# Hybrid decoder block in fp32 pieces: another issue order in the passage from the output projection to the up projection

## The chip, the core and the metric

The kernel runs on one core of one Trainium2 chip. The metric is the device time in microseconds. Five engines work side by side, each through its own list of instructions in a fixed order: TensorE (PE in the profile, with its weight loads as PEld), VectorE (DVE), ScalarE (ACT), GpSimd (POOL) and SyncE (SP, which here only issues transfers).

## What is computed

The reference is one transformer block on 512 tokens of width 1024, all in float32:

```python
h = rmsnorm(x, norm_attn_g)
u = h @ w_in                                    # q, k, v, pool input, gates
a = diff_attention(q, k, v, positions, lam, subln_g, lam_init)
p = multiscale_pool(u_pool, w_pool, pool_scale)
x = x + (sigmoid(g_A) * a + sigmoid(g_P) * p) @ w_out
h2 = rmsnorm(x, norm_mlp_g)
z = square(relu(h2 @ w_up))                     # 1024 -> 4096
x = x + z @ w_down                              # 4096 -> 1024
return rmsnorm(x, final_norm_g)
```

The change concerns the lines from `x + ... @ w_out` to the first part of `h2 @ w_up`.

## The kernel before, in words

**Products in three terms.** Every float32 operand is split into a high part (a cast to the multiplier's format, on ScalarE) and a low part (operand minus high part, on VectorE). A product is then three matmuls: high by high, high by low, low by high. For a weight tile of 128 by 1024 this split is `split_w`: the cast at L112, the subtraction at L113.

**Output projection.** `po` accumulates the left 512 output columns for four row tiles of 128 tokens (t = 0 to 3) in four PSUM banks at once (L605 to L610). The right 512 columns follow row tile by row tile in the loop from L625: 8 slices k of the inner dimension, three matmuls each (`mm_rows`, L581 to L583), into bank 4 + t. The four weight tiles `ws` of the right half are split just ahead of that loop (L619 to L622).

**What follows each row tile.** As soon as row tile t is finished, `x1_add` adds the residual (L587, VectorE) and squares with a row sum (L561, ScalarE). `row_scale` makes the inverse root of the mean square with one step of refinement (L571 to L573 on ScalarE, L574 and L575 on VectorE). L636 multiplies the row tile by its scale and by the gain: this is `h2`, in two buffers used in turn. Eight transposes on TensorE (L644, tile `h2T`) turn it into two PSUM banks with the features on the partitions.

**The up projection's forms.** The MLP's products use Strassen's scheme (Winograd's form): the inputs are split in two by features and in two by tokens, and seven products, called A11, A12, S1, S2, S3, A22 and S4, take the place of eight. A11 and A12 need the first two row tiles alone: their operands are the cast and the subtraction at L656 and L657. The other forms need row tiles 2 and 3 as well. For t = 2 and 3 the loop copies a transposed bank (L649), adds and subtracts (L650), and makes the operands of S1 and S2 (`forms_h2`, L596 for the difference, L602 for the cast, L603 for the low part).

**The products of `up(0)`.** `product` runs one form: for i in 0, 1 (two weight tiles, two output banks) and p in 0, 1 (halves of a bank) four high-by-high and high-by-low pairs (L775, L778) and then four low-by-high matmuls (L781), each with 256 columns. One form is 48 matmuls. In `up(0)` the order of the forms is A11, A12, S1, S2, S3, A22, S4. The weights come from the generator `weights`: A11's are block 0 (`b11`), A12's block 2 (`b21`), and S1's a sum in the buffer pair `ga`. `parts` does the splitting. For S1 its casts are ordered behind the last `row_scale` (L729). After S1's split the next block is added onto `ga` by an accumulating transfer that GpSimd issues (`plus`, L685): the sum is the weight of S2. Outputs of A11 are kept at L803, and A12's are added to them at L807 (`join`).

**What sets the order of the work.** The scheduler takes, for each engine, the ready instruction that stands earliest in the program, by a simulated clock of its own, and so writes down one fixed order per engine. `after(later, earlier)` adds a constraint for two instructions of one engine: in that engine's list the first comes behind the second. It adds no wait between engines. The constraints around the change are these, before:

- the first matmul of row tile t of the right half comes behind the last of row tile t - 1, for t = 1, 2, 3 (L629);
- the transposes of row tile 0 come behind the end of row tile 1's matmuls, those of row tile 1 behind the end of row tile 2's (L631 to L633);
- the transposes of row tile 2 come behind the second quarter of A11 (L785), those of row tile 3 behind the second quarter of A12 (L788);
- the casts of A11's and A12's weights (`b11`, `b21`, two tiles each) have no constraint.

Of the kernel before, what the change touches and what calls it, by code (L numbers as in the profile page):

```python
# [51 lines left out]
def block_kernel(ctx, tc, xT, x_tok, gains, pos, consts, w_in, w_v, w_pool, w_out, w_up, w_dn, out):  # L52
# [10 lines left out]
    state = {}  # L63
# [153 lines left out]
    for n in range(2):  # L217
        accs = [bank((0, 1, 2, 3, 4, 5, 6, 0)[4 * n + t], f"v{n}_{t}") for t in range(NT)]
        for kk in range(4):
# [7 lines left out]
            for k2 in range(2):  # L227
# [4 lines left out]
                k = 2 * kk + k2  # L232
# [11 lines left out]
            if n == 0 and 0 < kk < 3:  # L244
                i = kk - 1
# [287 lines left out]
    A11, A12, A22, A21, S1, S2, S3, S4 = range(8)  # L533
# [34 lines left out]
    def row_scale(t, n):  # L568

        src, r, u = (st[:, t, i : i + 1] for i in (n, 4, 5))  # L570
        A.activation(out=r, in_=src, func=AF.Ln, scale=1.0 / D, bias=st[:, t, 2:3])  # L571
        A.activation(out=r, in_=r, func=AF.Exp, scale=-0.5)
        state["rows"] = A.activation(out=u, in_=r, func=AF.Square, scale=1.0 / math.sqrt(D))  # L573
        V.scalar_tensor_tensor(out=u, in0=src, scalar=st[:, t, 3:4], in1=u, op0=ALU.add, op1=ALU.mult)  # L574
        V.scalar_tensor_tensor(out=r, in0=u, scalar=-3.0, in1=r, op0=ALU.add, op1=ALU.mult)  # L575
        return r
# [48 lines left out]
    for t in range(NT):  # L625
        a_ = bank(4 + t, f"po1_{t}")
        for k in range(NK):
            m, end = mm_rows(a_, t, k, ws[k // 2], k == 0, k == NK - 1)
            if t and k == 0:  # L629
                after(m, state["po"])  # L630
        if 0 < t < 3:  # L631
            for b in range(2):
                after(state["h2T", t - 1, b], end)  # L633
        state["po"] = end
        x1_add(t, 1, a_)
        V.scalar_tensor_tensor(out=h2[:, t % 2], in0=x1[:, t, :], scalar=row_scale(t, 1), in1=g2b, op0=ALU.mult, op1=ALU.mult)  # L636
        pv = []
        for b in range(2):
            pt = bank((t % 2) * 2 + b, f"h2T{t}_{b}")
            for j in range(4):  # L640
                k = 4 * b + j
                if j == 1:
                    state["h2T", t, b] = state["h2T"]
                state["h2T"] = T.transpose(out=pt[:, j * P : j * P + P], in_=h2[:, t % 2, k * P : k * P + P], identity=ident)  # L644
            pv.append(pt.rearrange("p (j q) -> p j q", q=P))
        sl = slice((t % 2) * P, (t % 2) * P + P)
        if t > 1:

            A.copy(out=hw[:, 1, :, sl], in_=pv[0])  # L649
            V.tensor_tensor(out=hw[:, 0, :, sl], in0=pv[1], in1=hw[:, 1, :, sl], op=ALU.subtract)  # L650
            forms_h2((S1, S2), sl)
        if t == 3:
            forms_h2((S3,), slice(0, HS))
        for b in range(t // 2, 2):
            hi, lo = (gab[b][:, t // 2, i, :, sl] for i in range(2))
            A.copy(out=hi, in_=pv[b])  # L656
            part = V.tensor_tensor(out=lo, in0=pv[b], in1=f(hi), op=ALU.subtract)  # L657
            if t == 3:
                after(part, state[S3])
            if t < 2:  # L660
                A.copy(out=h2f[:, b, :, sl], in_=pv[b])
# [8 lines left out]
    def weights(src, q, nm, order):  # L670

        def raw(b, tag="wr", pool=wp):
            if b == 2:
                both = big.tile([P, 2, 1024], F32, tag="s1b", name=f"wr21_{nm}{q}")
                tiles = [both[:, c] for c in range(2)]
            else:
                tiles = [pool.tile([P, 1024], F32, tag=tag, name=f"{tag}_{nm}{b}_{q}_{c}", bufs=2) for c in range(2)]
            if b is not None:
                for c in range(2):
                    nc.sync.dma_start(out=tiles[c], in_=src[q, b, c])  # L680
            return tiles

        def plus(tiles, b):

            return [G.dma_start(out=tiles[c], in_=src[q, b, c], accum_op=ALU.add) for c in range(2)]  # L685

        def parts(rs, b, hold=None, add=None):

            third = nparts[0] % 3 == 2
            nparts[0] += 1  # L690
            out_ = []
            for c in range(2):
                hi, lo = (
                    (bk if third else wp).tile([P, 1024], F32R, tag=t_ + "b" * third, name=f"{t_}_{nm}{b}_{q}_{c}", bufs=2 if third else 4)
                    for t_ in ("wh", "wl")
                )
                if add is None:
                    cast = split_w(rs[c], hi, lo, eng=V)
                else:

                    cast = A.copy(out=hi, in_=rs[c])
                    A.mul(out=lo, in_=f(hi), mul=-1.0)
                    G.dma_start(out=lo, in_=src[q, add, c], accum_op=ALU.add)
                if hold:
                    after(cast, hold)
                out_.append((hi, lo))
            return out_

        early = nm == "u" and q == 0
        r11, al, ga = raw(0), raw(1, "wal", bk), raw(None, "wga", bk)  # L710
        for c in range(2):
            if early:
                nc.sync.dma_start(out=ga[c], in_=src[q, 0, c])
            else:
                V.tensor_tensor(out=ga[c], in0=r11[c], in1=al[c], op=ALU.add)
        if early:
            plus(ga, 1)
            plus(al, 3)
        for n, form in enumerate(order):
            if form == A11:  # L720
                yield parts(r11, "b11", zhi[q, S1] if nm == "d" and q else None)
            elif form == A12:
                yield parts(raw(2), "b21", zhi[q, A11] if nm == "d" and q else None)
            elif form == S4:
                yield parts(raw(3), "b22", None, 3 if nm == "d" and q == 3 else None)
            elif form == S3:
                yield parts(al, "t3", first[-1])
            else:
                w = parts(ga, f"t{form}", state["rows"] if form == S1 and early else None if form == S1 else first[-1])  # L729
                if form != A22:  # L730
                    adds = plus(ga, {S1: 3, S2: 2}[form])
                if form == S1 and not early:

                    for i in plus(al, 3):
                        after(i, adds[1])
                yield w
# [23 lines left out]
    def up(q):  # L760
# [3 lines left out]
        def product(form, name, onto=None):  # L764
# [3 lines left out]
            for i in range(2):  # L768
                hi, lo = w[i]
                for p in range(2):  # L770
# [11 lines left out]
                        if q == 0 and form == A12 and (i, p, k) == (1, 0, 0):  # L782
                            after(m, state["h2T"])
                    if q == 0:
                        if (form, i, p) == (A11, 0, 1):  # L785
                            for b in range(2):
                                after(state["h2T", 2, b], m)
                        elif (form, i, p) == (A12, 0, 1):  # L788
                            for b in range(2):
                                after(state["h2T", 3, b], m)  # L790
                        if form != A11 or i + p:
                            after(begin, state["um"])
                        state["um"] = m
# [226 lines left out]
```

## Time and profile before

| what | before |
|---|---|
| median of three runs | 676.74 us (676.6 to 678.25) |
| the profiled execution's own time | 677.01 us |
| its span, first to last instruction | 675.1 us |
| PE busy | 664.3 us (98%) |
| DVE busy | 529.7 us (78%) |
| ACT busy | 461.6 us (68%) |
| POOL busy | 122.3 us (18%) |
| granted TensorE clock, mean | 0.997 |

All times in the views are microseconds from the start of the span. The stretch that the change touches runs from about 326 us (left half of the output projection ends) to about 371 us (third product of the up projection ends). Buffer numbers are left out of tile names: `po` is any of the output projection's banks, `um` any bank of an up product, `wh_ub` and `wl_ub` the high and low parts of a block's weights (`b11`, `b21`, `b22`), `wh_ut` and `wl_ut` those of a sum's weights (S1, S2 and so on), `gss` an operand of S1 to S4, `rawz` the buffer of kept products. In a row of the timeline the columns are start, duration, engine, line, operation, output and inputs, count, and in brackets the idle time of the engine ahead of it with what ended it. Matmuls follow one another every 0.12 us in `um` (256 columns) and every 0.23 us in `po` (512 columns).

### The profile page before, as it was taken

The page shows a single profiled execution, that of the slowest core. Times are in us where ns is not written, and L with a number is a line of the kernel's source. Part 1 is how long each engine was busy: PE and PEld are TensorE (multiplying, and loading weights), DVE is VectorE, ACT ScalarE, POOL GpSimd, SP SyncE. Part 2 cuts the span into 40 slices and gives each one's busy share as a digit, 9 for nine tenths or more (in the row PEclk, how much of TensorE's full clock was granted, in tenths as well). Part 3 has the DMA queues.
Part 4 walks back from the last instruction along what each step waited for, and adds up shares of the span by engine and source line. Part 5 has one row for each costly group of instructions (what it writes and reads, how often), then busy time and mean ns, then how long its engine had stood idle before and what let it go on. Part 6 is the DMA issues. An engine that isn't in the chain of part 4 may idle for free.

```text
span 675.1 us, 9993 instructions
## 1 busy us (share of the span) xinstructions
PE 664.3 (98%) x3686; PEld 579.5 (86%) x3686; DVE 529.7 (78%) x879; ACT 461.6 (68%) x741; POOL 122.3 (18%) x137
## 2 busy tenths in 40 slices
PE   9999999999999999999999999999999999999995
PEld 7788888888888888888789988899889998899884
DVE  6955877799979986975578998657994599747995
ACT  8464587978887698883577875367743696356874
POOL 6201110132133212520202020202103021210120
PEclk9999999999999999999999999999999999999998
DMA  7526464335254364574964697776959579493863
GB/s 274 188 69 184 126 152 125 102 94 126 86 141 107 98 169 96 127 192 175 306 197 84 198 218 187 167 191 142 234 183 195 195 155 259 129 212 130 214 125 124
DMA packets 32880, 109.34 MB, mean 162 GB/s; under 512 B 4032, under 2 KB 4928, under 8 KB 32832
## 3 DMA queue, kind: packets, MB, share of 16 engines
q0 software_dynamic: 10656, 38.80, 32.2%
q1 hardware_dynamic: 21744, 69.38, 29.1%
q8 instruction: 29, 0.48, 0.3%
q10 hardware_dynamic: 432, 0.52, 0.2%
q14 instruction: 19, 0.16, 0.1%
HBM read 106.59 MB, written 2.10 MB: 161 GB/s over the span
## 4 chain that ended last, share of the span: by engine, by line
PE 95%; DVE 2%; issue 1%; DMA 1%; ACT 1%; SPq 0%; DVEq 0%
PE um L778 8%; PE um L775 8%; PE um L781 8%; PE dm L865 7%; PE dm L867 7%; PE dm L868 7%; PE o L417 2%; PE ga L132 2%; PE ga L131 2%; PE gp L135 2%; PE k L132 2%; PE gp L132 2%; PE k L131 2%; PE gp L131 2%; PE k L135 2%; PE ga L135 2%
## 5 line engine op out<-in xcount | busy, mean ns | idle before, releaser
L778 PE MATMUL um<-gss,wh_ut 128*128 128x256 f32 x192 | 48.2, 284 | 1.3 <-DVE gss L603 1.3
L867 PE MATMUL dm<-wh_dt,z 128*128 128x512 f32 (+1 forms) x128 | 49.5, 386 | 0.0
L868 PE MATMUL dm<-wl_dt,z 128*128 128x512 f32 (+1 forms) x128 | 49.4, 386 | 0.0
L865 PE MATMUL dm<-wh_dt,z 128*128 128x512 f32 (+1 forms) x128 | 49.3, 387 | 0.0
L775 PE MATMUL um<-gss,wh_ut 128*128 128x256 f32 x192 | 48.2, 283 | 0.0
L883 DVE TENSOR_TENSOR x<-x,dm 128x512 f32<-128x512 f32 x48 | 32.7, 682 | 18.3 <-PE dm L868 18.2
L400 ACT ACTIVATE p<-p,st 128x128 f32<-128x128 f32 (+3 forms) x64 | 35.7, 559 | 14.1 <-DVE st L396 13.8
L685 POOL DMA_DIRECT2D wga_dNone<-w_dn x16 | 14.2, 885 | 154.5 <-DVE wl_dt L113 154.5
L112 ACT CAST wh_ut<-wga_uNone 128x1024 fp32r<-128x1024 f32 x24 | 24.7, 1050 | 25.1 <-PE dm L867 19.5
L112 ACT CAST wh_ub<-wr_u 128x1024 fp32r<-128x1024 f32 x24 | 25.1, 1049 | 22.6 <-PE um L778 13.5
L778 PEld LDWEIGHTS um<-gss,wh_ut 128*128 128x128 f32 x192 | 36.9, 192 | 1.5 <-DVE gss L603 1.5
L867 PE MATMUL dm<-wh_db,z 128*128 128x512 f32 x96 | 37.2, 389 | 0.0
L868 PE MATMUL dm<-wl_db,z 128*128 128x512 f32 x96 | 37.2, 389 | 0.0
L685 POOL DMA_DIRECT2D wga_uNone<-w_up x18 | 15.6, 864 | 117.8 <-DVE wl_ut L113 93.2
L775 PEld LDWEIGHTS um<-gss,wh_ut 128*128 128x128 f32 x192 | 36.9, 192 | 0.0
L865 PE MATMUL dm<-wh_db,z 128*128 128x512 f32 x96 | 35.9, 389 | 0.0
L113 DVE TENSOR_TENSOR wl_ub<-wr_u,wh_ub 128x1024 fp32r<-128x1024 f32 x24 | 29.2, 1220 | 8.4 <-ACT wh_ub L112 8.3
L113 DVE TENSOR_TENSOR wl_ut<-wga_uNone,wh_ut 128x1024 fp32r<-128x1024 f32 x24 | 28.7, 1221 | 8.1 <-ACT wh_ut L112 8.0
L750 DVE TENSOR_TENSOR z<-rawz,z 128x1024 fp32r<-128x1024 f32 x28 | 33.6, 1219 | 1.3 <-ACT z L747 1.3
L747 ACT CAST z<-rawz 128x1024 fp32r<-128x1024 f32 x28 | 28.6, 1045 | 7.0 <-PE dm L868 3.2
L396 DVE CUSTOM_DVE_ANT_0 p<-s,mask 128x128 f32<-128x128 f32 (+3 forms) x64 | 30.3, 484 | 3.4 <-PE s L395 3.3
L112 ACT CAST wh_dt<-wga_dNone 128x1024 fp32r<-128x1024 f32 x24 | 24.9, 1049 | 11.8 <-issue 5.1
(324 smaller groups left out, 2221.1 us busy)
## 6 DMA issues: line engine op xcount, KB each, us to landing
wr_u<-w_up SPq DMA_DIRECT2D x24, 512.0 KB, 5.4
wr_d<-w_dn SPq DMA_DIRECT2D x24, 512.0 KB, 4.3
wga_uNone<-w_up POOLq DMA_DIRECT2D x18, 512.0 KB, 6.7
wga_dNone<-w_dn POOLq DMA_DIRECT2D x16, 512.0 KB, 5.5
wr_k<-w_in SPq DMA_DIRECT2D x8, 512.0 KB, 3.3
wr_ga<-w_in SPq DMA_DIRECT2D x8, 512.0 KB, 3.3
wr_gp<-w_in SPq DMA_DIRECT2D x8, 512.0 KB, 4.0
wl_ga<-w_in POOLq DMA_DIRECT2D x8, 512.0 KB, 5.4
```

Source lines behind the costliest of these rows:

```text
L112: ins = A.copy(out=hi[:, sl], in_=raw[:, sl])
L113: (eng or G).tensor_tensor(out=lo[:, sl], in0=raw[:, sl], in1=f(hi)[:, sl], op=ALU.subtract)
L131: T.matmul(acc, lhsT=hi[:, c], rhs=rh[:, k, :], start=k == 0, stop=False)
L132: T.matmul(acc, lhsT=hi[:, c], rhs=rl[k], start=False, stop=False)
L135: T.matmul(acc, lhsT=lo[:, c], rhs=rh[:, k, :], start=False, stop=k == NK - 1)
L400: A.activation(out=pr[:, c, :N], in_=pr[:, c, :N], func=AF.Exp, scale=-1.0, bias=st[:, c : c + 1], accum_out=st[:, 2 + c : 3 + c])
L775: m = T.matmul(a_, lhsT=hi[:, c], rhs=rh[:, k, :], start=p + k == 0 and onto is None, stop=False, skip_group_check=True)
L778: T.matmul(a_, lhsT=hi[:, c], rhs=rl[:, k, :], start=False, stop=False, skip_group_check=True)
L781: m = T.matmul(a_, lhsT=lo[:, c], rhs=rh[:, k, :], start=False, stop=k == 3, skip_group_check=True)
L865: m = T.matmul(a_, lhsT=zh, rhs=hi[:, sl], start=p == 0 and start, stop=False, skip_group_check=True)
L867: T.matmul(a_, lhsT=zl, rhs=hi[:, sl], start=False, stop=False, skip_group_check=True)
L868: end = T.matmul(a_, lhsT=zh, rhs=lo[:, sl], start=False, stop=p == 3, skip_group_check=True)
```

## The change

Three edits, all of them constraints on the order. No instruction is added or removed.

- The first matmul of row tile 1 is no longer held behind the last of row tile 0. The scheduler may now mix the two.
- The cast of A11's second weight tile is put behind the last ScalarE step of row tile 1's `row_scale`; the casts of both of A12's weight tiles behind that of row tile 3's.
- The transposes of row tile 2 are put behind the end of row tile 3's matmuls instead of A11's second quarter; those of row tile 3 behind A11's last quarter instead of A12's second quarter.

```diff
@@ the loop over row tiles
             m, end = mm_rows(a_, t, k, ws[k // 2], k == 0, k == NK - 1)
-            if t and k == 0:
+            if t > 1 and k == 0:
                 after(m, state["po"])
-        if 0 < t < 3:
+        if t:
             for b in range(2):
                 after(state["h2T", t - 1, b], end)
         state["po"] = end
         x1_add(t, 1, a_)
         V.scalar_tensor_tensor(out=h2[:, t % 2], in0=x1[:, t, :], scalar=row_scale(t, 1), in1=g2b, op0=ALU.mult, op1=ALU.mult)
+        state["rows", t] = state["rows"]
@@ parts
                     G.dma_start(out=lo, in_=src[q, add, c], accum_op=ALU.add)
+                if early and (b, c) in (("b11", 1), ("b21", 0), ("b21", 1)):
+                    after(cast, state["rows", 1 if b == "b11" else 3])
                 if hold:
                     after(cast, hold)
@@ product in up
                     if q == 0:
-                        if (form, i, p) == (A11, 0, 1):
-                            for b in range(2):
-                                after(state["h2T", 2, b], m)
-                        elif (form, i, p) == (A12, 0, 1):
+                        if (form, i, p) == (A11, 1, 1):
                             for b in range(2):
                                 after(state["h2T", 3, b], m)
```

`early` is true for the weights of `up(0)` alone.

## The prediction

> **What bounds the kernel now.** I read the page first, then the chain of waits, then TensorE's waits, then the stretch around the change by stages.
>
> ```profile
> span 675.1 us, 9993 instructions
> PE 664.3 (98%) x3686; PEld 579.5 (86%) x3686; DVE 529.7 (78%) x879; ACT 461.6 (68%) x741; POOL 122.3 (18%) x137
> PE 95%; DVE 2%; issue 1%; DMA 1%; ACT 1%; SPq 0%; DVEq 0%
> ```
>
> TensorE sets the end: it is busy for 98% of the span and is 95% of the chain that ended last. An order of work can then gain only where TensorE stands still. Of its waits for other engines, two lie in the passage (total, times, longest; the rows left out belong to the kernel's first microseconds):
>
> ```profile
> PE um L778 <- DVE gss L603: 1.3, 1, 1.3
> ...
> PE po L582 <- DVE wl_o L113: 0.4, 1, 0.4
> ```
>
> The windows (stretch, then its length, then busy time and count of PE, PEld, DVE, ACT, POOL, then the granted clock, the DMA share and GB/s) show that nothing else there stands still:
>
> ```profile
> 328.50:331.05 2.55, 2.19 (x10) 1.49 (x8) 2.36 (x6) 2.37 (x6) 1.73 (x2) 1.00 0.96 318
> 331.05:337.90 6.85, 6.85 (x30) 5.68 (x31) 4.17 (x13) 3.51 (x10) 0.86 (x1) 1.00 1.04 246
> 337.90:350.40 12.50, 12.50 (x65) 10.53 (x64) 8.81 (x13) 9.08 (x20) 0.00 (x0) 1.00 0.68 177
> 350.40:363.66 13.26, 13.26 (x113) 13.22 (x112) 10.78 (x16) 9.81 (x21) 1.73 (x2) 1.00 0.65 156
> 363.66:365.21 1.55, 0.28 (x3) 0.08 (x2) 1.31 (x3) 1.05 (x3) 0.00 (x0) 1.00 0.04 8
> 365.21:370.97 5.76, 5.76 (x48) 5.76 (x49) 5.76 (x6) 5.26 (x8) 1.72 (x2) 1.00 0.35 51
> 371.00:400.00 29.00, 29.00 (x219) 27.90 (x219) 28.57 (x29) 24.98 (x33) 3.51 (x4) 1.00 0.78 197
> ```
>
> PE is full from 331.05 to 363.66, and again from 365.21, at full granted clock. The idle parts are 2.55 - 2.19 = 0.36 and 1.55 - 0.28 = 1.27 us. So the change can gain 1.63 us at most in the passage, 0.24% of 676.74. A matmul of `po` takes 6.85 / 30 = 0.23 us, one of `um` 5.76 / 48 = 0.12, so a quarter of a form 1.44 and a form 5.76. About 0.3%, 2.03 us, is what a measurement of this kernel can tell from no change.
>
> **First stall: row tile 0's last weights.** These are rows of the chain of waits (start, duration, what).
>
> ```profile
> 328.68 1.06 ACT wh_o L112
> 329.77 1.24 DVE wl_o L113
> 331.05 0.50 PE po L582
> ```
>
> The fourth weight tile of the right half is cast only at 328.68, when the left half's last matmul has left its buffer. Its low part comes 2.3 us later, at 331.01, and PE runs out of row tile 0's earlier slices 0.36 us ahead of that. With row tile 1 free to start, 6 of its 8 slices need only the first three weight tiles: 18 matmuls of 0.23 us, 4.1 us, against a hole of 0.36. Two matmuls fill it. If the scheduler puts more of them ahead of row tile 0's end, that end comes later by their time, but the transposes of row tile 0 do not suffer: they stand at 341.17 (below), row tile 0 ends before its L587 at 332.51, and the same work ends both row tiles at the same time. I take -0.36; the other end is 0, if the scheduler mixes nothing at that place.
>
> ```profile
> 332.51 0.69 DVE L587 TENSOR_TENSOR x<-po,x 128x512 f32<-128x512 f32 x1
> 341.17 1.03 PE L644 MATMUL h2T<-ident,h 128*128 128x128 f32 x8
> 347.96 1.03 PE L644 MATMUL h2T<-ident,h 128*128 128x128 f32 x8
> 355.70 1.04 PE L644 MATMUL h2T<-ident,h 128*128 128x128 f32 x8
> 359.92 1.04 PE L644 MATMUL h2T<-ident,h 128*128 128x128 f32 x8
> ```
>
> **Second stall: S1's low operand.** First a row of ScalarE's timeline, then VectorE's:
>
> ```profile
> 362.61 0.61 ACT L602 CAST gss<-hw 128x512 fp32r<-128x512 f32 x1
> ```
>
> ```profile
> 362.22 0.69 DVE L603 TENSOR_TENSOR gss<-hw,gss 128x512 fp32r<-128x512 f32 x1 [0.20 <-ACT gss L602]
> 363.87 0.69 DVE L807 TENSOR_TENSOR rawz<-um,rawz 128x512 f32<-128x512 f32 x1 [0.95 <-PE um L781]
> 364.47 0.68 DVE L603 TENSOR_TENSOR gss<-hw,gss 128x512 fp32r<-128x512 f32 x1
> ```
>
> Row tile 3's low part for S1 is the last L603. Its input, cast on ScalarE at 362.61, is there at 363.2. But in VectorE's list it stands behind the second join (L807), which waits for A12's last matmul. So PE waits for VectorE, and VectorE has idled 0.95 us for PE. The change moves row tile 3's transposes from A12's second quarter to A11's end: two quarters, 2 x 1.44 = 2.9 us earlier. Then the low part's input can be there near 360.3, and the second join cannot stand ahead of it unless the scheduler's clock lets it slip by 2.9 us. I take -1.27; the other end is 0.
>
> Are row tile 3's `h2` there by A11's end? These rows bear on it:
>
> ```profile
> 350.63 0.69 DVE L587 TENSOR_TENSOR x<-po,x 128x512 f32<-128x512 f32 x1
> 351.43 1.28 DVE L636 SCALAR_TENSOR_TENSOR h<-x,st,rawz 128x1024 f32<-128x1024 f32 x1
> 353.36 1.29 DVE L636 SCALAR_TENSOR_TENSOR h<-x,st,rawz 128x1024 f32<-128x1024 f32 x1
> 354.56 2.36 DVE L113 TENSOR_TENSOR wl_ut<-wga_uNone,wh_ut 128x1024 fp32r<-128x1024 f32 x2
> ```
>
> The second L636, row tile 3's, ends at 354.65, 0.36 earlier in the new kernel: 354.3. A11 begins near 350.4 - 0.36 = 350.0 and ends 5.76 + 1.04 (row tile 2's eight transposes, inside it or ahead of it) later, at 356.8. Yes, with 2.5 us in hand. Row tile 2's are no worse: today its `h2` waits for ScalarE and VectorE to do A12's casts first (below), and is ready at 352.7 only.
>
> **The casts that move.** A12's two weight tiles today are cast in the middle of row tile 2's scale (a step of it, L571, stands between the two casts):
>
> ```profile
> 345.72 1.03 ACT L112 CAST wh_ub<-wr_u 128x1024 fp32r<-128x1024 f32 x1
> 347.02 1.06 ACT L112 CAST wh_ub<-wr_u 128x1024 fp32r<-128x1024 f32 x1
> 346.79 2.54 DVE L113 TENSOR_TENSOR wl_ub<-wr_u,wh_ub 128x1024 fp32r<-128x1024 f32 x2 [1.73 <-ACT wh_ub L112]
> 352.67 0.20 ACT L573 ACTIVATE st<-st 128x1 f32<-128x1 f32 x1
> 352.78 1.98 ACT L112 CAST wh_ut<-wga_uNone 128x1024 fp32r<-128x1024 f32 x2
> ```
>
> Two casts and two subtractions go from there, where VectorE idled 1.73 us ahead of them, to behind row tile 3's L573. That place is today taken by S1's two casts and, on VectorE, by S1's two subtractions (354.56 to 356.92). A12's stand earlier in the program, so S1's are pushed back by at least another pair, 2.36 us on VectorE. Row tile 2's five operations (L650, L603, L657, L596, L603, each about 0.6 from start to start, as from 363.87 to 364.47) may also come ahead, since they no longer wait for late transposes. PE needs A12's first low part 8 matmuls after A12's start: 356.8 + 0.96 = 357.8. It is ready between 354.3 + 1.2 = 355.5 and, behind those five, 358.5. I take 0 and keep 0.7 for the range. A11's second tile moves from ahead of row tile 1's scale to behind it, past a few short steps that follow an L587 before row tile 2's end, and is first needed in A11's second half, 350.0 + 2.88: nothing.
>
> **What S1's late split makes late.** When S1's subtraction is done, the accumulating transfer for S2 starts, then S2's cast, then S2's subtraction. These rows of the transfer view have the time from issue to landing in the last column: first today's two transfers behind S1's split, issued one after the other; then two of the same kind near 330, beside three loads that SP issued (the fifth row, their median); then the down projection's two loads, which wait for the buffer of A12's weights and so move with its split:
>
> ```profile
> wga_uNone<-w_up POOLq DMA_DIRECT2D x1, 512.0 KB, 5.6
> wga_uNone<-w_up POOLq DMA_DIRECT2D x1, 512.0 KB, 7.9
> wga_uNone<-w_up POOLq DMA_DIRECT2D x1, 512.0 KB, 13.1
> wga_uNone<-w_up POOLq DMA_DIRECT2D x1, 512.0 KB, 12.3
> wr_u<-w_up SPq DMA_DIRECT2D x3, 512.0 KB, 8.1
> wr_d<-w_dn SPq DMA_DIRECT2D x1, 512.0 KB, 3.2
> wr_d<-w_dn SPq DMA_DIRECT2D x1, 512.0 KB, 4.2
> ```
>
> S1's second subtraction, today done at 356.92, ends between 354.3 + 2 x 2.36 = 359.0 and, with five operations of row tile 2, two of row tile 3 and a join ahead of it (8 x 0.6), 363.8. Add 7.9 and a cast of 1.03: S2's second high part is there at 367.9 to 372.7. PE starts S1 at 363.66 - 0.36 = 363.3, S2 5.76 later at 369.1, and needs that part after half a form, 371.9. So it is 4.0 early to 0.8 late. The first tile's split ends 1.2 sooner, at 357.8 to 362.6; with 5.6 and 1.03 its high part is there at 364.4 to 369.2, against 369.1. The down projection's loads now start when A12's split is done, 354.3 + 2.36 = 356.7 at the soonest, take 3 to 4 us and so share the engines with these transfers for a part of their time. I take a new wait of 0.3 us ahead of or inside S2, near the late end because row tile work has the precedence; ends 0 and 2 (0.8, and another 1.2 for the shared engines). The Trainium skill prices such a transfer lower: its page "DMA: Bandwidth & Descriptors", section "Anatomy of one DMA — SWDGE (gpsimd) path", fits about 2.0 us plus the bytes over 436 GB/s, for 512 KB an estimate of 3.2 us. By that S2's weights would have 2.4 to 4.7 us more, the term would be 0 and the sum -1.63; the trace's 5.6 and 7.9 for this accumulating kind speak against it.
>
> **Sum.** -0.36 - 1.27 + 0.3 = -1.33 us on the profiled execution's 677.01 us: 675.68. The median shown, 676.74, is 0.27 below that execution, so I forecast 675.4 us. From 371 to 400 PE is full (29.00 of 29.00, the last window above) and the waits name no other place behind the passage, so what is gained at 371 arrives at the end.
>
> **The rivals.**
>
> *A. The second stall stays.* If the scheduler again writes the join ahead of row tile 3's low part, only 0.36 is gained: 676.4. For it: its clock counts the chain from a row tile's end to its transposes as long. It placed row tile 0's at 341.17, 8.7 us behind the L587 at 332.51, where row tile 3's `h2` ends 4.0 us behind its L587 (350.63 to 354.65). Against it: the 2.9 us, and the casts that leave row tile 2's and 3's chain.
>
> *B. A12's weights come late.* VectorE does row tile 2's five operations first, and A12 waits up to 0.7 us for its first low part; with S2's 0.3 to 1.0 on top, 0.6 to nothing of the 1.63 is left: 676.1 to 676.8. For it: VectorE is 10.78 of 13.26 us busy from 350.40 to 363.66 already, and gets 2.36 us more. Against it: the 1.28 of row tile 2's L636 leaves that stretch.
>
> *C. Slower.* One mechanism: S2's accumulating transfers run beside the down projection's loads and take what they took at 330, 12.3 to 13.1 us. From a first split at 360.2, the middle of its bounds, S2's first high part is then ready at 360.2 + 13.1 + 1.03 = 374.3 instead of 369.1: PE waits 5.2, and the sum is -1.63 + 5.2 = +3.6: 680.3. It decides against the change once that part is later than 369.1 + 1.63 = 370.7, that is from a transfer of 9.5 us. For it: the loads do move into that time. Against it: they took 3.2 and 4.2 us and there are two, while near 330 three loads at 8.1 were on the way.
>
> *D. The change does not mix the row tiles.* Then 0.36 stays, and with the rest as forecast the time is 675.8; this lies in the forecast's own range, 675.0 to 676.0.
>
> *E. More than 2.03 us is gained.* No row of the passage has it to give. It needs a better order further on, or luck of the measurement: the runs before spread by 678.25 - 676.6 = 1.65 us. A time of 674.5 stands for it.
>
> **How the numbers follow.** Forecast with D 0.52, A 0.14, B 0.14, C 0.11, E 0.09. Faster by over 0.3% (below 674.7) is E and an edge of the forecast: 0.11. Slower by over 0.3% (above 678.8) is C and an edge of B: 0.13. The rest, 0.76, is within. For 8 times in 10 the range takes the full 1.63 with some spread of runs at the low end, 674.6, and at the high end B with its worst terms, a wait of 2 us at S2 and a part of the way to C: 678.3.
>
> **What would show it.** The wait of L582 for `wl_o` is gone, and `po` rows run on through 331. The transposes of row tiles 2 and 3 begin near 351 to 353 and 356.8 to 358.5. VectorE's last L603 for S1 comes ahead of the second L807, and PE's wait for `gss` is gone. `wh_ub` casts stand behind 352. If I am wrong in the large, the windows show it as a new PE wait for `wh_ut` or `wl_ut` between S1 and S2 (C), or for `wl_ub` in A12 (B). A PE that is as full as I say but slower in its matmuls, or a wait after 371, would be something that I have not seen at all.

## The result: slower by half a per cent

| | before | after |
|---|---|---|
| median | 676.83 us (676.6 to 678.25, 6 runs) | 680.32 us (679.39 to 681.7, 6 runs) |
| ratio, 95% interval | | 1.0048 [1.0035, 1.0062] |
| profiled execution, its span | 677.01, 675.1 us | 681.7, 679.2 us |
| PE busy | 664.3 us | 666.4 us |

The forecast was 675.4 us with a range of 674.6 to 678.3. The change is slower, and its 680.32 us lies outside that range.

**What to compare.** The two profiles differ by 4.1 us of span, but 1.37 of that lies ahead of the passage, where the order of work is the same. The last output group (L417) starts at 304.55 before and 305.92 after. So I measure the *stretch*: from that start to the last matmul into `dm4b`, the up and down products' last bank, near the kernel's end. First two rows of the timeline of before, then two of after:

```profile
304.55 0.81 PE L417 MATMUL o<-wt,vh 128*128 128x512 f32 x4
667.66 0.28 PE L868 MATMUL dm4b<-wl_dt,z 128*128 128x256 f32 x1
```

```profile
305.92 0.81 PE L417 MATMUL o<-wt,vh 128*128 128x512 f32 x4
671.81 0.28 PE L868 MATMUL dm4b<-wl_dt,z 128*128 128x256 f32 x1
```

Before it is 667.66 - 304.55 = 363.11 us, after 671.81 - 305.92 = 365.89: 2.78 longer. To lay a time of the profile after beside one of before, take 1.37 from it ("aligned" below; the other runs are aligned by their own start of that group). The median differs by 3.49, 0.7 more than the stretch. About 0.5 of that lies outside the spans: the six device times after are longer than their spans by 2.07 to 2.50 us (median 2.41), where the profiled execution before is longer than its own by 1.91 and the later runs of that kernel by 1.83 to 1.99. The remaining 0.2 is far within the spread of the six runs of a kernel, 1.7 to 2.3.

**The profile after.** TensorE's waits that bear on the passage (total, times, longest):

```profile
PE um L781 <- DVE gss L603: 2.2, 2, 1.3
PE um L778 <- DVE rawz L807: 1.5, 2, 0.9
```

The wait of `po` for `wl_o` is gone, the one for `gss` is there twice instead of once, and a new pair is named for `rawz`, the joins' output. The windows with the prediction's limits:

```profile
328.50:331.05 2.55, 2.55 (x13) 2.12 (x12) 2.46 (x4) 0.99 (x2) 1.75 (x2) 1.00 1.03 421
...
371.00:400.00 29.00, 26.54 (x208) 25.43 (x207) 28.46 (x28) 25.01 (x35) 4.39 (x6) 1.00 0.70 178
```

TensorE is full at 328.50 now. But from 371 to 400 it stands still for 29.00 - 26.54 = 2.46 us where it was full before. The places, from TensorE's timeline:

```profile
365.95 0.39 PE L781 MATMUL um<-gss,wh_ut 128*128 128x256 f32 x1 [1.27 <-DVE gss L603]
...
372.99 0.39 PE L781 MATMUL um<-gss,wh_ut 128*128 128x256 f32 x1 [0.95 <-DVE gss L603]
...
385.55 0.39 PE L778 MATMUL um<-gab,wh_ut 128*128 128x256 f32 x1 [0.63 <-DVE rawz L807]
389.55 0.39 PE L778 MATMUL um<-gab,wh_ut 128*128 128x256 f32 x1 [0.87 <-DVE rawz L807]
```

The first is S1's second matmul, with the same 1.27 as before. The second is the same place in S2. The last two are the two halves of A22, whose output banks must first be emptied by S3's two joins (L807). VectorE's timeline says why:

```profile
355.97 2.35 DVE L113 TENSOR_TENSOR wl_ub<-wr_u,wh_ub 128x1024 fp32r<-128x1024 f32 x2
358.24 1.22 DVE L113 TENSOR_TENSOR wl_ut<-wga_uNone,wh_ut 128x1024 fp32r<-128x1024 f32 x1
...
360.58 1.22 DVE L113 TENSOR_TENSOR wl_ut<-wga_uNone,wh_ut 128x1024 fp32r<-128x1024 f32 x1
...
362.31 0.69 DVE L651 TENSOR_TENSOR hw<-h2T,hw 128x512 f32<-128x512 f32 x1
...
364.60 0.69 DVE L807 TENSOR_TENSOR rawz<-um,rawz 128x512 f32<-128x512 f32 x1 [0.40 <-PE um L784]
365.21 0.68 DVE L603 TENSOR_TENSOR gss<-hw,gss 128x512 fp32r<-128x512 f32 x1
...
368.63 1.22 DVE L113 TENSOR_TENSOR wl_ut<-wga_uNone,wh_ut 128x1024 fp32r<-128x1024 f32 x1 [2.02 <-ACT wh_ut L112]
371.11 1.22 DVE L113 TENSOR_TENSOR wl_ut<-wga_uNone,wh_ut 128x1024 fp32r<-128x1024 f32 x1 [1.25 <-ACT wh_ut L112]
372.25 0.68 DVE L603 TENSOR_TENSOR gss<-hw,gss 128x512 fp32r<-128x512 f32 x1
```

A12's pair of subtractions now stands at 355.97, and S1's two behind it, at 358.24 and 360.58. The second of them stands ahead of row tile 3's sum (L651, 362.31), so that row tile's low part for S1 (L603, 365.21) is again behind A12's second join. Then VectorE idles for 2.02 and 1.25 us: S2's weights are late. The rows of ScalarE and of GpSimd for them:

```profile
367.56 1.05 ACT L112 CAST wh_ut<-wga_uNone 128x1024 fp32r<-128x1024 f32 x1 [2.89 <-DMA wga_uNone<-w_up]
...
370.03 1.05 ACT L112 CAST wh_ut<-wga_uNone 128x1024 fp32r<-128x1024 f32 x1 [0.37 <-DMA wga_uNone<-w_up]
370.98 0.62 ACT L602 CAST gss<-hw 128x512 fp32r<-128x512 f32 x1
```

```profile
359.76 0.86 POOL L686 DMA_DIRECT2D wga_uNone<-w_up  x1 [23.46 <-DVE wl_ut L113]
362.10 0.86 POOL L686 DMA_DIRECT2D wga_uNone<-w_up  x1 [1.47 <-DVE wl_ut L113]
```

Before, GpSimd issued these accumulating transfers at 356.08 and 357.21, so in aligned time they go out 2.31 and 3.52 us later. They took 7.8 and 7.9 from issue to landing (before 5.6 and 7.9), and land at 367.5 and 370.0. S2's operand cast (L602) stands behind the second weight cast in ScalarE's list, its low part (L603) behind the subtraction in VectorE's: that is the 0.95 in S2.

**What a wait costs.** The idle time in brackets is less than the loss. Before, S1's first matmul starts at 363.66 and these two follow:

```profile
365.21 0.39 PE L778 MATMUL um<-gss,wh_ut 128*128 128x256 f32 x1 [1.27 <-DVE gss L603]
365.43 0.28 PE L775 MATMUL um<-gss,wh_ut 128*128 128x256 f32 x1
```

The second starts 1.55 behind the first where 0.12 is usual, so 1.43 late; and the third follows after 0.22 instead of 0.12. Together 1.53, for an idle time of 1.27. By such starts the changed profile loses 1.53 in S1 (as before), 1.29 in S2, 0.27 ahead of S3's second half, 0.89 and 1.12 in A22, and gains the first stall, by its starts 0.63 (before, 330.30 to 331.05 and on to 331.39, where 0.23 is usual): 1.29 + 0.27 + 0.89 + 1.12 - 0.63 = +2.94. The stretch shows +2.78.

### The profile page after: what moved, and what is told of

It reads as the page before. It is cut to its first block, busy times and chain, and to the rows that moved or that the text cites. A ratio compares the mean times of both kernels' runs of the same rounds, so it can differ in the third digit from the quotient of the medians.

```text
span 679.2 us, 9991 instructions
## 1 busy us (share of the span) xinstructions
PE 666.4 (98%) x3686; PEld 581.3 (86%) x3686; DVE 529.2 (78%) x879; ACT 461.2 (68%) x741; POOL 122.4 (18%) x137
## 4 chain that ended last, share of the span: by engine, by line
PE 88%; DMA 5%; issue 3%; DVE 3%; ACT 1%; SPq 0%; POOLq 0%
PE dm L865 7%; PE dm L867 7%; PE dm L868 7%; PE um L778 6%; PE um L784 6%; PE um L781 6%; DMA wga_uNone<-w_up 5%; PE v L235 2%; PE v L236 2%; PE v L237 2%; PE o L417 2%; PE ga L132 2%; PE ga L131 2%; PE gp L135 2%; PE gp L132 2%
## 5 line engine op out<-in xcount | busy, mean ns | idle before, releaser
L750 ACT CAST z<-rawz 128x1024 fp32r<-128x1024 f32 x28 | 28.6, 1046 | 6.7 <-PE dm L868 3.2
```

## The experiments

All expectations count with the same stretch, or, in the first four, with the *passage*: from the same start to the first matmul of the down projection, 89.59 us before. Ratios are to the kernel before, run again beside each experiment, so they are not the quotients of the medians in this table. A stretch is of one execution. The median span of a kernel's runs differs from that of before by the same amount within about 0.5 us; a smaller difference between two stretches says little without the rows.

| run | what it holds | median us | ratio [95%] | stretch us |
|---|---|---|---|---|
| before | | 676.83 | | 363.11 |
| after | edits 1, 2, 3 | 680.32 | 1.0048 [1.0035, 1.0062] | 365.89 |
| mix_only | 1 | 676.84 | 0.9995 [0.9983, 1.0007] | 363.52 |
| casts_only | 2 | 680.6 | 1.0052 [1.0031, 1.0073] | 367.09 |
| transposes_only | 3 | 677.38 | 1.0008 [0.9997, 1.0019] | 363.53 |
| mix_transposes | 1, 3 | 677.46 | 1.0008 [0.9997, 1.0019] | 363.28 |
| half_casts | 1, 3, half of 2 | 678.2 | 1.0015 [1.0006, 1.0024] | 364.80 |
| after_no_transfer | after, S2's sum left out | 678.02 | 1.0015 [1.0006, 1.0024] | 363.63 |
| after_loads_late | after, down's loads later | 680.13 | 1.0038 [1.0024, 1.0052] | 365.99 |
| after_low | after, S1's low part first | 679.99 | 1.0039 [1.0025, 1.0052] | 365.96 |
| before_join | joins first | 677.08 | 1.0003 [0.9991, 1.0015] | 362.94 |
| after_join | after, joins first | 678.47 | 1.0019 [1.001, 1.0028] | 364.58 |
| mix_transposes_join | 1, 3, joins first | 676.51 | 0.9991 [0.9982, 1.0] | 362.26 |
| best_keep | 1, 3, joins and keep first | 674.64 | 0.9961 [0.9948, 0.9973] | 360.79 |
| before_keep | joins and keep first | 677.72 | 1.0001 [0.9991, 1.001] | 362.96 |
| after_keep | after, joins and keep first | 677.91 | 1.0009 [0.9999, 1.0018] | 363.97 |

### The three edits one by one

`mix_only` is before with the first edit, `casts_only` with the second, `transposes_only` with the third, `mix_transposes` with the first and the third:

```diff
# mix_only
-            if t and k == 0:
+            if t > 1 and k == 0:
# casts_only
+                if early and (b, c) in (("b11", 1), ("b21", 0), ("b21", 1)):
+                    after(cast, state["rows", 1 if b == "b11" else 3])
# transposes_only
-        if 0 < t < 3:
+        if t:
...
-                        if (form, i, p) == (A11, 0, 1):
-                            for b in range(2):
-                                after(state["h2T", 2, b], m)
-                        elif (form, i, p) == (A12, 0, 1):
+                        if (form, i, p) == (A11, 1, 1):
```

> Edit: row tile 1 may mix with row tile 0, nothing else. I measure the passage from the start of the attention's last group of o matmuls (L417) to the first down matmul (L865): 89.6 us before (304.55 to 394.14), 92.4 us with the whole change (305.92 to 398.29). Theory (A12's casts behind row tile 3 delay S1's split, and with it S2's transfer): the first stall goes, the wait for S1's low operand stays at 1.3 us: passage 89.0, time 0.6 us under before. Rival (mixing itself does harm): passage over 90.

> Edit: only the three casts are held behind the row scales. Theory: this edit carries the loss; S1's second split ends 2.4 us later or more, S2 waits about 1 us, A22's joins are late: passage 91.5 to 93, time 2 to 3.5 us over before. Rival (the earlier transposes do it): passage within 0.5 us of 89.6.

> Edit: only the other places of the transposes of row tiles 2 and 3. Theory: no loss, the passage between 88.2 (second stall gone) and 89.8 (it stays). Rival (earlier transposes put row work ahead of the weights' splits): passage 91 or more and S2's transfers issued over 2 us later than before.

> Edit: mixing and transposes, without the held casts. Theory: passage 87.6 to 89.2, time 0.4 to 2 us under before, S2's transfers issued within 1 us of before. Rival (it takes more than the casts): passage over 90.

`mix_only`: the first stall is gone, and nothing is gained; the passage is 90.01, by 0.42 longer. TensorE's waits and two rows of VectorE:

```profile
PE um L778 <- DVE gss L603: 1.3, 1, 1.3
...
PE um L775 <- DVE rawz L807: 0.9, 1, 0.9
```

```profile
366.81 1.23 DVE L113 TENSOR_TENSOR wl_ut<-wga_uNone,wh_ut 128x1024 fp32r<-128x1024 f32 x1 [0.87 <-ACT wh_ut L112]
...
384.63 0.68 DVE L807 TENSOR_TENSOR rawz<-um,rawz 128x512 f32<-128x512 f32 x1
```

TensorE is earlier, VectorE is not: it waits 0.87 for the cast of S2's second weight tile, and S3's second join starts at 384.63, aligned 385.08 and so 0.42 later than before. A22's second half waits 0.87 where it waited for nothing. (A part is this run's own: S2's second transfer took 9.2 there against 7.9 before. But in `mix_transposes`, with 7.9, the same wait is again 0.87.) Before, the join was just in time. First the join on VectorE, then A22's second half on TensorE, both before the change:

```profile
384.66 0.69 DVE L807 TENSOR_TENSOR rawz<-um,rawz 128x512 f32<-128x512 f32 x1
```

```profile
384.87 0.64 PE L781 MATMUL um<-gab,wl_ut 128*128 128x256 f32 x4
385.41 0.39 PE L775 MATMUL um<-gab,wh_ut 128*128 128x256 f32 x1
```

Four matmuls at 0.12 end the first half's feed at 384.87 + 0.48 = 385.35, the join ends at 384.66 + 0.69 = 385.35, and the second half starts at 385.41: no reserve at all. It is 0.06 late and its next step is 0.10 longer than 0.12, so this place already costs 0.16.

`transposes_only` and `mix_transposes` say the same more strongly. S1's stall is gone in both, as forecast for the edit of the transposes, and A22 waits instead. In `mix_transposes` TensorE has neither of the two old stalls, and in their place these:

```profile
PE um L775 <- DVE rawz L804: 1.2, 2, 0.9
...
PE um L775 <- ACT rawz L800: 0.5, 1, 0.5
```

L804 there is the join (L807 before), L800 the copy that keeps S2's output (`keep`, L803 before). Of the 2.2 us that the stalls cost, 0.6 for the first and 1.5 for the second, all but nothing arrives: the stretch is 363.28.

`casts_only` is the slow one: 1.0052, as slow as all three together. Its down projection's first product comes ahead in TensorE's list, so the passage can't be read; the longest wait is that product's for ScalarE, 2.1 us, and a fall of the granted clock behind it (last section) is in the time too. Of its four runs the one with the highest mean clock, 0.997 against 0.995, took 679.43 us, still 2.6 above before. S1 and S2 wait there too, for `gss`, but only 0.38 and 0.44. The other two edits by themselves cost nothing that can be measured, so the loss comes with the edit of the casts.

### How the held casts cost: a half dose, no transfer, no shared engines

`half_casts` holds only the second of A12's two casts (and A11's). `after_no_transfer` leaves out the accumulation that makes S2's weights: S2 works with S1's, without a transfer. `after_loads_late` issues the two loads of down's first weights behind those of its next block. All three otherwise have the change's order.

```diff
# half_casts
-                if early and (b, c) in (("b11", 1), ("b21", 0), ("b21", 1)):
+                if early and (b, c) in (("b11", 1), ("b21", 1)):
# after_no_transfer
-                if form != A22:
+                if form == S1 and early:
+                    adds = []
+                elif form != A22:
# after_loads_late
+                    if nm == "d" and q == 0 and b == 2:
+                        after(load, state["wal_d"])
```

> Edit: the change, but of A12's two casts only the second is held behind row tile 3's scale. Theory (each cast behind row tile 3 pushes S1's split, and so S2's transfers, by about 1.2 us): stretch midway, 364.0 to 365.2, between 363.3 (mixing and transposes alone) and 365.9 (the change). Rival (the loss comes from A11's held cast or from a chance order): 363.3 or 365.9.

> Edit: the whole change, but without the two accumulating transfers that turn S1's weights into S2's in the first up projection; S2 then works with S1's weights, so this part of the computation is changed. I measure the stretch from the attention's last group of o matmuls to the last down matmul of the kernel: 363.1 us before, 365.9 with the change. Theory (late transfers hold S2's casts, these hold VectorE, and VectorE's list then brings A22's joins late): S2's wait for gss and both waits of A22 for the join go, the wait at S1 stays: stretch 362.3 to 363.2. Rival (VectorE has simply too much to do there, whatever the transfers): A22's waits stay and the stretch is over 365.

> Edit: the whole change, but the down projection's two loads that ran beside S2's transfers are issued by SP behind the next pair of loads, some 16 us later. Theory: the first of S2's transfers takes 5.6 us again instead of 7.8, the second, which sets the wait, stays between 5.6 and 7.9; S2's wait shrinks by no more than 1 us; stretch 364.9 to 365.9. Rival C of the prediction (sharing the engines makes the loss): the second transfer lands 2 us sooner and the stretch is under 364.

Half the dose gives a bit over half the loss: 364.80 stands 1.52 above `mix_transposes`, the full change 2.61 above it. But the way there is not the one expected. In aligned time S2's second transfer lands at 368.87, as late as in the whole change (368.64), and S2 waits for nothing. These are the waits:

```profile
PE um L778 <- ACT rawz L803: 1.3, 1, 1.3
PE um L781 <- DVE gss L603: 1.3, 1, 1.3
```

The second is S1's, at full length. The first is S3's wait for ScalarE's copy that keeps S2's output: in ScalarE's list it stands behind a cast of A22's weights, which at 378.36 had waited 1.70 for its transfer. A third, of 0.69, is the down projection's. So the time in the middle is no proof of a loss in proportion to the casts. In `after_no_transfer` S2's and A22's waits are gone, and 365.89 falls to 363.63, somewhat short of the 362.3 to 363.2 expected: S1's wait of 1.27 stays, and a wait of 1.05 of S3 for ScalarE's keep of S2 comes up. So some 2.3 of the 2.78 go through the transfers.

`after_loads_late` looks as if sharing the DMA engines didn't matter: 365.99, as slow as the change. Its transfers took 5.4 and 5.6 instead of 7.8 and 7.9, and S2's wait is gone, but A22 waits 1.77 for its first join, since VectorE's and ScalarE's work on down's late loads now stands ahead of it (ScalarE idles 2.95 for them). And something else is in that time, which the windows show:

```profile
384.00:386.00 2.00, 0.76 (x7) 0.56 (x5) 2.00 (x3) 2.00 (x3) 0.00 (x0) 1.00 0.00 0
386.00:388.00 2.00, 1.47 (x8) 1.47 (x9) 2.00 (x3) 2.00 (x5) 0.00 (x0) 0.75 0.49 168
388.00:390.00 2.00, 2.00 (x12) 2.00 (x11) 1.88 (x2) 0.54 (x2) 0.00 (x0) 0.50 0.39 141
390.00:392.00 2.00, 2.00 (x17) 2.00 (x17) 0.20 (x1) 1.28 (x2) 0.86 (x1) 0.90 0.86 244
```

Behind the wait the granted clock falls to 0.50, for (0.25 + 0.50 + 0.10) x 2 = 1.7 us of lost work. Of its ten runs, the four with a mean clock of 0.996 or more took 678.13 to 678.97 us, the six below that 680.01 to 681.64; the profile is of one of the six. With the 1.7 taken off the stretch is 364.3, between the theory's 364.9 and the rival's 364. The time by itself decides for neither side; the transfers speak for the rival, as S2's second one lands at 366.35 aligned, 2.3 sooner than in the changed kernel. So the sharing with down's loads does cost, and the order of the loads alone doesn't bring it back.

### S1's low part first

`after_low` is the changed kernel with S1's last low part (L603) ahead of A12's second join, which is what the prediction expected of the change itself.

```diff
+            if form == S1:
+                state["low", "S1"] = state[form]
...
+            if q == 0:
+                after(state["join"], state["low", "S1"])
```

> Edit: the whole change, and on VectorE A12's second join behind row tile 3's low part of S1. Theory (TensorE's wait at S1 is only that order; but VectorE then idles for S2's late transfers all the same): the wait of 1.3 us at S1 goes, S2's wait for gss and A22's waits grow by about as much, stretch (last group of o matmuls to last down matmul) 365.4 to 366.2, against 365.9. Rival (a wait on TensorE is worth its length): stretch 364.4 or less.

S1's wait falls from 1.27 to 0.17, and the stretch stays at 365.96. The transfers land when they land, whatever TensorE does, and S2's operand stands in ScalarE's and VectorE's lists behind the weights that they bring. So S2 waits 1.39 and 0.44 instead of 0.95: by the starts of the matmuls 1.1 us gained in S1 and 1.0 lost in S2. The wait has moved, as the theory had it. But the time is no proof of it, because behind these two waits the clock falls here too:

```profile
370.00:372.00 2.00, 0.89 (x4) 0.69 (x5) 2.00 (x3) 2.00 (x5) 0.86 (x1) 0.97 0.93 127
372.00:374.00 2.00, 2.00 (x11) 2.00 (x11) 1.97 (x3) 2.00 (x3) 0.00 (x0) 0.50 1.03 195
374.00:376.00 2.00, 2.00 (x14) 2.00 (x14) 2.00 (x2) 1.37 (x3) 0.00 (x0) 0.68 1.07 223
```

(0.03 + 0.50 + 0.32) x 2 = 1.7 us. VectorE used that time to catch up: A22's first wait and S3's, 0.89 and 0.27 in the changed kernel, are gone, and A22's second is 0.90 instead of 1.12. With the 1.7 taken off, the stretch would be 364.3, on the rival's side; with those 0.89 + 0.27 + 0.22 = 1.38 put back, 365.6, on the theory's. So what it would be at the full clock can't be told from this run.

### What VectorE and ScalarE do behind the passage

If VectorE's list paces TensorE up to A22, then a shorter list ahead of S3's joins must pay where a stall was removed, and only there. The down projection's first VectorE work (the weights' sum L715, the low part of z L750, the subtractions of `wl_db`) stands between those joins. `before_join`, `after_join` and `mix_transposes_join` put it behind both.

```diff
+                if nm == "d" and q == 0:
+                    after(add_, state["join", 0])
...
+        if q == 0 and form == A11:
+            after(low, state["join", 0])
...
+                    if nm == "d" and q == 0 and ("join", 0) in state:
+                        after(state["low"], state["join", 0])
```

> Edit: the kernel before, with the down projection's work on VectorE behind both joins of S3. Theory (before, the joins were just in time and TensorE's two stalls are as they were): no change, stretch 362.9 to 363.3. Rival (the new order of the joins alone is the gain): 362.3 or less.

> Edit: the whole change, and the same order of the joins. Theory: of the change's waits only A22's go (1.1 us at the second join, some of 0.9 at the first): stretch 364.0 to 365.0. Rival: no gain, over 365.5.

> Edit: mixing and transposes without the held casts, and on VectorE the work for the down projection (its weight sums and splits, A11's low part of z) put behind both joins of S3. Theory (what TensorE gained earlier was given back because A22 waits for S3's second join, which stands behind three such operations on VectorE): A22's wait of 0.9 us goes, stretch 361.2 to 362.4, 0.7 to 1.9 under before. Rival (VectorE's total work sets the pace): the wait moves to A22's end or to the first down product, stretch 363 or more.

On the kernel before it is worth 0.17 us, about the 0.16 by which A22's second half was late there; on `mix_transposes` 1.02, on the changed kernel 1.31. All three lie where the theory had them. What remains in `mix_transposes_join` is S3's wait of 0.62 for ScalarE's keep of S2's output, and 0.32 for the first join.

`best_keep` therefore also puts that keep ahead of the casts of A22's weights and of S4's second weight tile:

```diff
+                if early and (b == f"t{A22}" or b == "b22" and c == 1):
+                    after(cast, state["keep", 0])
```

> Edit: mixing, transposes, joins ahead, and on ScalarE the keeping of S2's outputs ahead of the casts of A22's weights and of S4's second weight tile, because S3 then waited 0.62 us for that copy. Theory: this wait goes and A22's 0.32 for the first join too; stretch 361.2 to 362.0, against 362.3. Rival (VectorE's list sets the pace, the wait moves on): stretch 362.2 or more.

No wait of TensorE is left in the passage. All the waits that its view shows are these three, in the first microseconds:

```profile
PE warm L170 <- POOL onesr L159: 1.1, 1, 1.1
PE v L235 <- ACT wh_v L112: 0.8, 1, 0.8
PE v L237 <- DVE xlb L185: 0.5, 1, 0.5
```

The median is 674.64 us (674.33 to 675.19), 0.9961 of before: faster than both kernels. The stretch is 2.32 shorter than before, a little better than expected (361.2 to 362.0).

Two runs then cross this order with the edits. `before_keep` has the order and no edit, `after_keep` the order and all three.

> The order of best_keep's joins and keeps (down's work on VectorE behind both joins of S3; on ScalarE S2's keep ahead of the casts of A22's and of S4's second weights) on the kernel before, with none of the change's edits. If the gain of best_keep is made of the stalls that edits 1 and 3 take away, and the order of joins and keeps only stops VectorE and ScalarE from giving it back, then both first stalls stay here: the stretch is best_keep's 360.79 plus 0.63 (first stall with its refill) plus 1.53 (second): 362.9, as with the joins alone (362.94) and 0.2 below before; ratio 0.999 to 1.001. The rival, that the keeps' order makes the gain and the change's two edits are worth nothing, expects 361.5 or less.

> The same order on the changed kernel, so with the casts of A12's weights held. If the held casts cost by themselves, through S1's split and the accumulating transfers for S2, then S1's wait of about 1.3 and S2's of about 1.0 stay and the ones at S3 and A22 go: best_keep's 360.79 plus 1.53 plus 1.29: 363.6, ratio 1.000 to 1.002. The rival, that the held casts cost only what VectorE's and ScalarE's later order makes of them, expects 361.5 or less.

`before_keep` is at 362.96, against 362.9 expected: the order alone is worth 0.15. Its waits are the two old ones, unchanged:

```profile
PE um L786 <- DVE gss L603: 1.3, 1, 1.3
...
PE po L582 <- DVE wl_o L113: 0.4, 1, 0.4
```

So the first and the third edit are worth 362.96 - 360.79 = 2.17 us once VectorE and ScalarE don't give it back. By the starts of the matmuls the second stall is 1.53 of that and the first 0.63, though only 1.63 of idle time was to be seen. And `after_keep`, at 363.97, shows that the held casts cost 363.97 - 360.79 = 3.18 us by themselves: its list of waits begins

```profile
PE um L789 <- DVE gss L603: 2.2, 2, 1.3
...
PE um L786 <- DVE rawz L815: 0.2, 1, 0.2
```

which is S1's and S2's pair of the changed kernel. By the starts, S1's 1.53, S2's 1.2 and a rest at A22 of 0.5 make up the 3.18. Not tried was a version with the casts held and S1's weights split ahead of A12's.

## Why the prediction was wrong

By the starts of the matmuls the terms came out like this: first stall -0.63 (forecast -0.36), second stall 0 (-1.27), S2 +1.29 (+0.3), S3 and A22 +2.28 (the forecast had nothing there). Together that is +2.94 instead of -1.33.

**First stall: right, the size too small.** TensorE runs full through 331, and `po` no longer waits. The term was -0.36; what the edit is worth is -0.63. The same holds for a stall of 1.27, worth 1.53. The idle time in the profile leaves out the modelled tail of the matmul before (0.28 where the next could follow after 0.12) and the slower first step behind it (0.22 for 0.12).

**Second stall: the term fell.** "I take -1.27; the other end is 0": the other end came, by the mechanism of rival A (the join again ahead of the low part), but for a reason that rival A didn't name. Row tile 3's transposes did move, to 358.73, or 357.36 aligned, inside the 356.8 to 358.5 that the prediction gave. `transposes_only` and `mix_transposes` have no S1 stall. The held casts brought it back: A12's pair and S1's two subtractions now stand ahead of row tile 3's sum (355.97 to 362.31 in VectorE's rows above). The prediction pushed these back by 2.36 in the step on S2 and forgot them in this one.

**S2: late as feared, but by another path, and more.** S1's split late, the transfers late, a wait in S2: all there. The term was +0.3, bounds 0 and 2; measured are 1.29 in S2 itself. S1's second subtraction ended at 360.58 + 1.22 = 361.80, 360.43 aligned, early in the bounds of 359.0 to 363.8. The transfer's 7.9 was right for the second one, but the first took 7.8 instead of 5.6. The prediction gave the sharing with down's loads 1.2; it cost 2.2 on the first transfer. And the path was another. The prediction reckoned with S2's second weight tile, but that was in time: its high part was there at 370.03 + 1.05 = 371.08 and its low part at 371.11 + 1.22 = 372.33, and S2, begun at 371.69, could not need them before 371.69 + 2.88 = 374.57. What TensorE waited for was the low part of S2's operand, which stood in the lists behind that tile's cast and its subtraction (371.11). The Trainium skill's fit of 2.0 us plus the bytes over 436 GB/s ("DMA: Bandwidth & Descriptors", "Anatomy of one DMA — SWDGE (gpsimd) path"), 3.2 us by estimate, doesn't fit any of these: 5.0 is the shortest time of such a transfer of up's weights in any run here.

**"What is gained at 371 arrives at the end": the step that failed in principle.** The prediction concluded it from TensorE's 29.00 of 29.00 from 371 to 400. The same row has VectorE at 28.57 of 29.00, and that was passed over. VectorE's list had no reserve before S3's second join (385.35 against 385.35), so anything gained ahead was given back as a wait there (`mix_only`, `mix_transposes`; in the second a part went to ScalarE's keep of S2), and anything late in S2 went on to A22 (0.89 and 1.12 in the changed kernel, of which `after_join` gets 1.31 back).

**The rivals.** A: its stall stayed, its time of 676.4 didn't hold, as S2's wait came on top. B: nothing to see of A12's weights; no wait for `wl_ub` is in the view. C: its 680.3 meets the measured 680.32, but for another reason. It wanted transfers of 12 to 13 us and a wait of 5.2 in S2; there are 7.8 and 7.9, and 1.29, and the rest is S1's stall that stayed and the joins. That its time came out is luck. D and E: no.

**The chances.** "Slower" had 0.13. A and the long form of S2's wait were priced as if only one could come; the pushed splits caused both.

## What to carry to other kernels

A TensorE that is full shows that the others are in time, not by how much: before costing an edit at what it frees, look up in the other engines' lists when the next result that TensorE needs was ready, and where the list ahead of it had no idle time. A batch of work that is held back is behind everything that the list now puts ahead of it and ahead of everything that follows; go through every consumer of that list with the same shift, not only through the one that was in mind. An edit that gains nothing alone may be worth its full price once the next list in the chain has room: here 2.17 us, found by ordering VectorE's and ScalarE's later work by what TensorE needs first.

## What the runs showed of the hardware

**The granted clock fell after about 2 us without work.** In `after_low`, `after_loads_late` and `casts_only` the clock went to about half for 3 to 4 us, worth 1.7 us each. Ahead of it TensorE had idled 1.83 us in two waits (1.39 and 0.44), 1.77 in one, and 2.12 in one. The rows of `casts_only`:

```profile
384.00:386.00 2.00, 0.70 (x6) 0.50 (x5) 2.00 (x3) 1.72 (x2) 0.00 (x0) 1.00 0.00 0
386.00:388.00 2.00, 1.18 (x5) 1.00 (x6) 2.00 (x4) 1.94 (x5) 0.00 (x0) 1.00 0.43 104
388.00:390.00 2.00, 2.00 (x9) 1.67 (x8) 2.00 (x2) 0.62 (x1) 0.00 (x0) 0.52 0.52 174
390.00:392.00 2.00, 2.00 (x13) 2.00 (x13) 0.06 (x1) 0.00 (x0) 0.86 (x1) 0.62 0.87 260
```

A single wait of 1.27 (before) or 1.29 us (`half_casts`) didn't do it, nor did the changed kernel's 0.63 and 0.87 within 5 us. The Trainium skill ("TensorE: Matmul & The Clock Gate", "HAM oscillation — how this bites in real kernels") warns of idle gaps of more than about 3.4 us, the length of the window by which the clock is set. Half rate for one such window would cost 1.7 us, an estimate from that figure, and these runs lost 1.7, so the length agrees; the bound doesn't, since 1.77 us of idle time were enough in the profiled run. But the length of a wait alone may not decide: four of the ten runs of `after_loads_late` had a mean clock of 0.996 or more and were over 1 us faster. Their waits aren't known. Where the bound lies between 1.3 and 1.77 us, and whether it depends on where in a window the wait falls, stays open.

**The start of the kernel.** The 1.37 us ahead of the passage belong to a slow start of the profiled execution after. The first group of four matmuls at L235, in the timeline of before and of after:

```profile
5.20 1.43 PE L235 MATMUL v<-wh_v,xh 128*128 128x512 f32 x4 [0.28 <-ACT wh_v L112]
```

```profile
5.72 2.07 PE L235 MATMUL v<-wh_v,xh 128*128 128x512 f32 x4 [0.80 <-ACT wh_v L112]
```

It waits 0.52 longer. Then the matmuls follow one another every 0.43 us until about 10 us, where before they did every 0.23 from 6.5 us on (the granted clock is given as 1.00 in both). The second group at L235 starts at 10.59 instead of 8.29, 2.30 later; 1.37 of that is left at 305.
